# A decoder step on one core: the sample tokens' attention, one sequence at a time, between the column blocks of the first half's up projection

## The chip, the cores and the metric

The kernel runs on one core of one Trainium2 chip. The metric is the device time of one execution in microseconds (us), as a median over runs. Short names of the engines: PE is TensorE (the matmuls), PEld its weight loads, DVE VectorE, ACT ScalarE, POOL GpSimd, SP SyncE, which here only starts DMAs. Each engine works through its own list of instructions in order; an instruction that has to wait holds up all that stand behind it in that list. PSUM is the memory that matmuls write to, SBUF the one that they read from.

## What is computed

One layer of a hybrid decoder, for a prompt of 1024 tokens and for 8 sampled sequences of 4 new tokens each (32 sample tokens). Shortened:

```python
proj = x @ w_in                                    # q, k, v | HGRN2's four parts | two gates
oa = diff_attention(q, k, v)                       # prompt: causal over its own 1024 keys
# sample: over 1024 cached keys and values in pages of 128, then the 4 new ones
k_past = cache_k[page_table].reshape(Bs, past_len, N_HEADS_A, 2, HEAD_DIM_A)
v_past = cache_v[page_table].reshape(Bs, past_len, N_HEADS_A, 2 * HEAD_DIM_A)
oa = diff_attention(qa, (k_past, ka), (v_past, va), sample_masks, lam)
ob = hgrn2_scan(...)
merged = sigmoid(ga) * (oa @ w_branch_a) + sigmoid(gg) * (ob @ w_branch_b)
h = layer_norm(ALPHA * x + merged @ w_out)
a, g = split(h @ w_up)                             # 2 x 2816 columns
y = (gelu(causal_conv3(a) + b) * g) @ w_down
out = layer_norm(ALPHA * h + y)
```

`diff_attention` is the difference of two softmaxes per head, 4 heads of 2 x 64 columns. The sample tokens' attention needs nothing of the prompt, and its result is first used in the second half of the tokens (below), in `oa @ w_branch_a`.

## The kernel before

Large matmuls are float32 split into a high and a low part (`split`, lines 129 to 131: ACT writes the high part, DVE the rest), and each product is three matmuls: high by high, high by low, low by high (`mm3`, `mm3s`; lines 225 to 227 and 235 to 237). Weights come through `wunit`: SP loads 512 KB into one of two `raw` buffers (line 142), ACT makes a tile `wh`, DVE a tile `wl`, of each of which five exist.

The program runs input projection, HGRN2 and prompt attention over all tokens, and then merge, up projection, down projection for two halves of the tokens: first prompt tokens 0 to 511, then prompt tokens 512 to 1023 with the 32 sample tokens. The up projection (`ffn`) is a loop over 22 column blocks m of 128. A block takes 48 matmuls for `a` (weights `wa`), a convolution on DVE, a Gelu on ACT, 48 matmuls for the gate (`wg`), a product and a split on DVE into the pair `u`. In the first half the blocks m < 16 do two chunks of 256 tokens (96 matmuls of 128x256 per block), the others one chunk of 512 (48 of 128x512). The pairs u0 to u15 lie in the pool `up`, u16 to u21 in `f3`.

Between the first half's merge and its up projection stands `sample_attn`, for two groups of 4 sequences. In a group, for each sequence j (a key step): POOL gathers the sequence's cached keys in two page buffers `pg` of 1 MB by indirect DMA (line 713); four DVE block transposes turn them into the one buffer `pw` (line 738); 64 small matmuls of 32x256 on 32x32 tiles of the array take them against the queries `q2` (line 744), which POOL copies into place, 16 copies per group (line 730). Scores of four steps stay in four PSUM buffers. Then the softmax (lines 748 to 760), a scaling by matmul that also turns the weights (lines 766, 769), the new tokens' share (line 777), and for each sequence a value step: two gathers into `pg` or into the halves of `pw`, and 32 matmuls on 128x32 tiles (line 789; two records each). At last a norm, a transpose (line 207) and a DMA to `osc` (line 807).

The order is not written out by hand: a scheduler with its own model of time places each engine's instructions by the order of the code, by what they need and by when buffers come free. So parts of the up projection already stand between the steps of `sample_attn` in the kernel before: blocks m < 16 need none of the buffers that `sample_attn` holds. The pools are stacks at two sides of SBUF: `z` (weights of `w_out`, later rows of the layer norm), `f1` (rows of x, line 942), `ap` (all buffers of `sample_attn`) and `f3` take turns at the right side.

The last step of the merge is `turn_`: for each tile of 128 tokens 8 transposes on PE (line 207), scale and shift on DVE and ACT (lines 957, 959), and the split into `hh` and `hl` (lines 130, 131), which the up projection reads.

Of the kernel before, what the change touches and what calls it, by code (L numbers as in the profile page):

```python
# [7 lines left out]
F32 = mybir.dt.float32  # L8
# [7 lines left out]
D = 1024  # L16
KD = 8
TP = 1024
TS = 32
T = TP + TS  # L20
NT = 9
DFF = 2816
NM = 22
# [22 lines left out]
def hybrid_step(ctx: ExitStack, tc: tile.TileContext, I, O):  # L46
# [49 lines left out]
    class Slots:  # L96
        def __init__(self, n):
            self.free = list(range(n))
            self.of = {}
# [606 lines left out]
    def sample_attn(ap):  # L706
        crow = {nm: I[nm].rearrange(pat, r=4) for nm, pat in (
            ("cache_k", "a l (p r) h m d -> (a l p) (r h m d)"), ("cache_v", "a l (p r) h e -> (a l p) (r h e)"))}

        def pages(dst, nm, b, c):  # L710

            i = b * 2 + c
            G.indirect_dma_start(dst.rearrange("p r e -> p (r e)"), None, crow[nm], bass.IndirectOffsetOnAxis(ap=idx[:, i:i + 1], axis=0))

        def half():
            return ap.tile([128, 4, 512], F32, tag="pg", name="pg", bufs=2)

        def whole():
            return ap.tile([128, 8, 512], F32, tag="pw", name="pw")

        q2 = ap.tile([128, 4, 4, 160], F32, name="q2")
        G.memset(q2, 0.0)
        qw = q2.rearrange("p c h (j x) -> p c h j x", x=40)
        for g in range(2):
            for c in range(4):
                src = qsm[c * 32:c * 32 + 32, :, g * 16:g * 16 + 16].rearrange("p h (j s) -> p h j s", j=4)
                for a in range(4):
                    G.tensor_copy(qw[a * 32:a * 32 + 32, c, :, :, (c // 2) * 4:(c // 2) * 4 + 4], src)  # L730
            sc = [ps_s.tile([128, 512], F32, tag="s", name="ps_s")[:, :256] for _ in range(2)] + [pst()[:, :256] for _ in range(2)]
            for j in range(4):
                kT = whole().rearrange("p x y -> p (x y)").rearrange("p (k q t) -> p k q t", k=16, t=32)
                for f in range(2):
                    kp = half()
                    pages(kp, "cache_k", g * 4 + j, f)
                    for r in range(0, 4, 2):
                        V.transpose(kT[:, :, f * 4 + r:f * 4 + r + 2].rearrange("p k q t -> p q k t"),  # L738
                                    kp[:, r:r + 2].rearrange("p q (k t) -> p q k t", t=32))
                for c in range(4):  # L740
                    for a in range(4):
                        ra = slice(a * 32, a * 32 + 32)
                        for hh in range(4):
                            PE.matmul(sc[a][hh * 32:hh * 32 + 32], lhsT=q2[ra, c, hh, j * 32:j * 32 + 32],
                                      rhs=kT[ra, hh * 4 + c].rearrange("p q t -> p (q t)"),
                                      start=(j + c == 0), stop=(j + c == 6))
            Pg = ap.tile([128, T], F32, tag="Pg", name="Pg")
            S.copy(Pg[:, TP:T], sn[:, g])
            Pv = Pg[:, :TP].rearrange("p (q a t) -> p q a t", q=8, a=4)
            for a in range(4):  # L750
                evac("sv"[a % 2], Pv[:, :, a], sc[a].rearrange("p (q t) -> p q t", t=32))
            mx = ap.tile([128, 8], F32, tag="mx", name="mx", bufs=2)
# [6 lines left out]
            Cg = ap.tile([128, 128], F32, tag="Cg", name="Cg")  # L759
            V.tensor_scalar(Cg, selC, mx[:, 7:8], None, ALU.mult)  # L760
            aT = ap.tile([128, 8, 128], F32, tag="aT", name="aT")
# [8 lines left out]
            an = ap.tile([TS, 128], F32, tag="an", name="an")  # L770
            evac("v", an, p[:TS, :128])

            po = pst()
            pov = po.rearrange("p (j e) -> p j e", j=4)
            for hh in range(4):
                hr = slice(hh * 32, hh * 32 + 32)
                PE.matmul(pov[hr], lhsT=an[:, hr], rhs=vs_[:, None, hh * 128:hh * 128 + 128].to_broadcast([TS, 4, 128]), start=True, stop=False)
            for j in range(4):
                if j % 2:
                    w = whole()  # L780
                    vps = [w[:, :4], w[:, 4:]]
                else:
                    vps = [half(), half()]
                for f in range(2):
                    pages(vps[f], "cache_v", g * 4 + j, f)
                for q in reversed(range(8)):
                    for hh in range(4):
                        hr = slice(hh * 32, hh * 32 + 32)
                        PE.matmul(pov[hr, j], lhsT=aT[:, q, hr], rhs=vps[q // 4][:, q % 4, hh * 128:hh * 128 + 128],
                                  start=False, stop=(j == 3 and q == 0))  # L790
            osb = ap.tile([128, 128], F32, tag="osb", name="osb", bufs=2)
# [6 lines left out]
            sq = ap.tile([128, 128], F32, tag="sq", name="ssq_")  # L798
# [6 lines left out]
            oc = ap.tile([128, 4, 16], F32, tag="soc", name="soc")  # L805
# [93 lines left out]
    def load_o(th, nh):  # L899
        Ot = [hilo(up, f"u{k}") for k in range(8)]  # L900
        for k in range(8):
            raw = wide(("hs", "ae")[k % 2])
            SY.dma_start(raw[:, :nh], osc[k, :, th:th + nh])
            split(raw[:, :nh], Ot[k][0][:, :nh], Ot[k][1][:, :nh])
        return Ot

    def zt(i, dt=F32R):

        return zp.tile([128, (2, 2, 2, 1)[i], D], dt, tag=f"z{i}", name=f"z{i}")
# [94 lines left out]
    def ffn(half, th, nh, tiles, cks, H, f3):  # L1004
# [3 lines left out]
        U = []  # L1008
        for m in range(NM):
            wa, wg = w_A(w_up, m * 128), w_A(w_up, DFF + m * 128)  # L1010
# [42 lines left out]
            U.append(u)  # L1053
        lnrow, rt01, rt23, rt4 = (zt(i, F32) for i in range(4))
# [3 lines left out]
        bst = zp.tile([128, 5, KD, 6], F32, tag="bst2", name="bst2")  # L1058
# [76 lines left out]
        return ln2  # L1135

    def rpool(name):
        return tc.tile_pool(name=name, bufs=1, side="right")
# [5 lines left out]
    with rpool("z") as zp:  # L1144
        H = merge(Ot, *HALVES[0])
    with rpool("ap") as ap:
        sample_attn(ap)
    with rpool("z") as zp:
        with rpool("f3") as f3:
            ln2 = ffn(0, *HALVES[0], H, f3)  # L1150
            Ot = load_o(*HALVES[1][:2])
        ln2(0, 4)
        H = merge(Ot, *HALVES[1])
        with rpool("f3") as f3:
            ffn(1, *HALVES[1], H, f3)

# [91 lines left out]
```

## Time and profile before

| | |
|---|---|
| time, median of 3 runs | 1828.04 us (1822.92 to 1828.65) |
| the profiled execution's own time | 1826.89 us |
| its span, first to last instruction | 1825.1 us |
| mean granted TensorE clock | 0.987 |
| busy: PE, DVE, ACT, POOL | 97%, 57%, 41%, 11% of the span |
| first half's up projection starts on PE | at 826.48 us |
| `sample_attn` on PE, first to last matmul | 851.13 to 1007.17 us |
| the stretch in which both share PE | 826.48 to 1013.71 us |

Times within the trace are counted from the span's start. The granted clock is the share of TensorE's full clock (2.4 GHz) that its throttle let through; in this trace it is 1.00 or 0.50 (1.2 GHz) at any moment, and a mean in between says for how long it was the one or the other. The profile's busy time of PE counts modelled ends of matmuls, so a busy PE can still be a slow one: how fast it works is read from the number of matmuls in a stretch.

### The profile page before, as it was taken

Reading aid. Unit: us, or ns where it says so; the run is one execution under the profiler, and the core shown is the slowest. Engines: PE = TensorE matmul, PEld = TensorE weight load, DVE = VectorE, ACT = ScalarE, POOL = GpSimd, SP = SyncE. Lnnn points to the kernel's source line nnn. Section 1 sums busy time; section 2 is a strip of 40 time slices with the busy share of each in tenths; the row PEclk is TensorE's granted clock in tenths of the full one; section 3 lists DMA queues with packets and bytes.
Section 4 is the critical chain, followed back from the end, with each engine's and each line's share of the span. In section 5 each row is a group of like instructions: output and inputs, shape, how many; then the busy total and the mean of one; then the engine's idle time right before and its main releaser. Section 6 shows DMA issues by size and latency. Waiting matters only on the chain.

```text
span 1825.1 us, 33731 instructions
## 1 busy us (share of the span) xinstructions
PE 1769.4 (97%) x13652; PEld 1657.4 (91%) x13652; DVE 1036.4 (57%) x2199; ACT 747.7 (41%) x1774; POOL 200.7 (11%) x280
## 2 busy tenths in 40 slices
PE   8999999999999999998898999999899999999996
PEld 8999999999999999887687998888887999999996
DVE  5757646764656553657454555434856555554336
ACT  6466354445553544334223333323325434343223
POOL 1000110120211010003321000000500000000113
PEclk9999999999999999999889999999999999999998
DMA  6110211221211223725677433333643323232224
GB/s 203 46 60 26 82 61 41 91 62 61 87 62 64 63 67 123 255 93 175 225 259 273 124 94 93 99 96 107 210 135 93 105 82 93 84 91 85 87 88 125
DMA packets 234832, 199.37 MB, mean 109 GB/s; under 512 B 8050, under 2 KB 213106, under 8 KB 230562
## 3 DMA queue, kind: packets, MB, share of 16 engines
q1 hardware_dynamic: 218432, 140.92, 25.7%
q0 software_dynamic: 9296, 47.44, 7.0%
q10 hardware_dynamic: 6948, 8.86, 1.4%
q8 instruction: 107, 1.75, 0.4%
q14 instruction: 49, 0.40, 0.1%
HBM read 173.00 MB, written 24.19 MB: 108 GB/s over the span
## 4 chain that ended last, share of the span: by engine, by line
PE 85%; DMA 5%; DVE 5%; issue 2%; ACT 1%; POOL 1%; SPq 0%; POOLq 0%; DVEq 0%; ACTq 0%
PE mm L237 13%; PE mm L236 12%; PE mm L235 12%; PE mm L225 11%; PE mm L227 10%; PE mm L226 10%; PE tp L207 3%; DMA pg<-in_cache_k_dram,idx 3%; PE tp L662 2%; PE sb L405 2%; PE mm L246 1%; PE scp L635 1%; PE scp L634 1%; DVE pw L738 1%; PE mx L225 1%
## 5 line engine op out<-in xcount | busy, mean ns | idle before, releaser
L131 DVE TENSOR_TENSOR wl<-raw,wh 128x512 fp32r<-128x512 f32 (+1 forms) x404 | 287.8, 717 | 359.6 <-ACT wh L130 339.7
L130 ACT CAST wh<-raw 128x512 fp32r<-128x512 f32 (+1 forms) x404 | 244.8, 611 | 498.2 <-PE mm L236 389.3
L236 PE MATMUL mm<-hl,wh 128*128 128x256 f32 (+2 forms) x1312 | 386.5, 295 | 1.6 <-DVE mv L893 1.4
L235 PE MATMUL mm<-hh,wh 128*128 128x256 f32 (+2 forms) x1312 | 384.8, 294 | 3.3 <-ACT hh L130 2.7
L237 PE MATMUL mm<-hh,wl 128*128 128x256 f32 (+2 forms) x1312 | 386.9, 295 | 0.0
L235 PEld LDWEIGHTS mm<-hh,wh 128*128 128x128 f32 x1312 | 247.9, 189 | 11.1 <-ACT hh L130 3.5
L236 PEld LDWEIGHTS mm<-hl,wh 128*128 128x128 f32 x1312 | 247.4, 189 | 9.0 <-issue 2.6
L237 PEld LDWEIGHTS mm<-hh,wl 128*128 128x128 f32 x1312 | 247.5, 189 | 6.0 <-issue 1.6
L225 PE MATMUL mm<-xh,wh 128*128 128x384 f32 (+1 forms) x560 | 187.1, 334 | 0.4 <-ACT wh L130 0.3
L226 PE MATMUL mm<-xl,wh 128*128 128x384 f32 (+1 forms) x560 | 186.8, 334 | 0.0
L227 PE MATMUL mm<-xh,wl 128*128 128x384 f32 (+1 forms) x560 | 186.0, 332 | 0.0
L225 PE MATMUL mm<-wh,xh 128*128 128x256 f32 x480 | 136.5, 285 | 0.7 <-DVE rb L578 0.7
L226 PE MATMUL mm<-wl,xh 128*128 128x256 f32 x480 | 136.3, 284 | 0.2 <-DVE wl L131 0.2
L227 PE MATMUL mm<-wh,xl 128*128 128x256 f32 x480 | 135.9, 283 | 0.0
L225 PEld LDWEIGHTS mm<-xh,wh 128*128 128x128 f32 x560 | 105.4, 188 | 3.8 <-issue 2.3
L227 PEld LDWEIGHTS mm<-xh,wl 128*128 128x128 f32 x560 | 105.4, 188 | 1.8 <-issue 1.5
L226 PEld LDWEIGHTS mm<-xl,wh 128*128 128x128 f32 x560 | 105.5, 188 | 1.2 <-issue 0.8
L225 PEld LDWEIGHTS mm<-wh,xh 128*128 128x128 f32 x480 | 90.2, 188 | 1.4 <-issue 0.9
L226 PEld LDWEIGHTS mm<-wl,xh 128*128 128x128 f32 x480 | 90.4, 188 | 0.5 <-DVE wl L131 0.4
L1068 POOL TENSOR_TENSOR c<-hh,hl 128x512 f32<-128x512 f32 (+2 forms) x24 | 22.7, 948 | 616.9 <-DVE u20l L131 391.3
L227 PEld LDWEIGHTS mm<-wh,xl 128*128 128x128 f32 x480 | 90.5, 188 | 0.1
L203 ACT COPY s<-tp 128x512 f32<-128x512 f32 (+3 forms) x96 | 39.4, 426 | 100.8 <-PE tp L207 42.6
(673 smaller groups left out, 3786.9 us busy)
## 6 DMA issues: line engine op xcount, KB each, us to landing
raw<-in_w_up_dram SPq DMA_DIRECT2D x88, 512.0 KB, 3.8
raw<-in_w_in_dram SPq DMA_DIRECT2D x44, 512.0 KB, 3.9
raw<-in_w_down_dram SPq DMA_DIRECT2D x36, 512.0 KB, 3.5
raw<-in_w_out_dram SPq DMA_DIRECT2D x16, 512.0 KB, 3.6
raw<-in_w_down_dram SPq DMA_DIRECT2D x18, 384.0 KB, 3.1
gsc<-gt ACTq DMA_DIRECT2D x32, 192.0 KB, 1.9
raw<-in_w_branch_b_dram SPq DMA_DIRECT2D x16, 256.0 KB, 4.1
raw<-in_w_branch_a_dram SPq DMA_DIRECT2D x16, 256.0 KB, 4.0
```

Of the source, the lines that this page charges most:

```text
L130: S.copy(h, src)
L131: eng.tensor_tensor(l, src, h.bitcast(F32), ALU.subtract)
L203: S.copy(out, in_)
L207: PE.transpose(out, in_, ident[:n, :n])
L225: PE.matmul(ps, lhsT=ah, rhs=bh, start=(i == 0), stop=False)
L226: PE.matmul(ps, lhsT=ah, rhs=bl, start=False, stop=False)
L227: PE.matmul(ps, lhsT=al, rhs=bh, start=False, stop=(i == n - 1))
L235: PE.matmul(ps, lhsT=ah, rhs=bh, start=(k == 0), stop=False)
L236: PE.matmul(ps, lhsT=ah, rhs=bl, start=False, stop=False)
L237: PE.matmul(ps, lhsT=al, rhs=bh, start=False, stop=(k == n - 1))
L405: PE.matmul(p[:, a * 64:a * 64 + 64], lhsT=W[:, a * 128:a * 128 + 128], rhs=rhs[:, a * nb:a * nb + nb], start=True, stop=True)
L662: PE.matmul(po[:, :128], lhsT=aT[:, j * 128:(j + 1) * 128], rhs=v_[:, j], start=(j == 0), stop=(j == i))
```

## The change

`sample_attn` becomes a class with the steps as methods: `keys(b)` and `values(b)` for one sequence b of 8, `soft(g)` at the end of a group's fourth key step, `out(g)` after its fourth value step. `ffn` takes a function that it calls behind each column block; in the first half this is `beside(m)`: behind the blocks 1, 2, 4, 5, 6, 8, 9, 10 one key step each, behind the blocks 12, 13, 15, 16, 17, 19, 20, 21 one value step each.

The buffers: the page buffers `pg`, and the softmax weights `aT` and `an` of both groups (two buffers of each), lie in a new pool `av` at the left side, where `z` was, and stay to the end of the up projection; `q2` and `pw` lie in `ap` at the right side, where `f1` was, and are given back behind block 10. Values come through `pg` alone. The softmax's scores `Pg` use `pw`. `z` moves to the left side, `f3` is opened at block 16. The instructions and their number stay the same but for this: values go through page buffers in rising order of rows.

```diff
-    def sample_attn(ap):
...
-        for g in range(2):
...
-            for j in range(4):
-                kT = whole().rearrange("p x y -> p (x y)").rearrange("p (k q t) -> p k q t", k=16, t=32)
-                for f in range(2):
-                    kp = half()
-                    pages(kp, "cache_k", g * 4 + j, f)
...
-            for j in range(4):
-                if j % 2:
-                    w = whole()
-                    vps = [w[:, :4], w[:, 4:]]
-                else:
-                    vps = [half(), half()]
...
+    class SampleAttn:
...
+        def pages(self, nm, b, c):
+
+            dst = self.av.tile([128, 4, 512], F32, tag="pg", name="pg", bufs=2)
...
+        def keys(self, b):
+            g, j = b // 4, b % 4
+            q2 = self.q2
+            if j == 0:
...
+                        G.tensor_copy(qw[a * 32:a * 32 + 32, c, :, :, (c // 2) * 4:(c // 2) * 4 + 4], src)
+                self.sc = [ps_s.tile([128, 512], F32, tag="s", name="ps_s")[:, :256] for _ in range(2)] + [pst()[:, :256] for _ in range(2)]
+            kT = self.whole().rearrange("p (k q t) -> p k q t", k=16, t=32)
+            for f in range(2):
+                kp = self.pages("cache_k", b, f)
+                for r in range(0, 4, 2):
+                    V.transpose(kT[:, :, f * 4 + r:f * 4 + r + 2].rearrange("p k q t -> p q k t"),
+                                kp[:, r:r + 2].rearrange("p q (k t) -> p q k t", t=32))
...
+            if j == 3:
+                self.soft(g)
...
+        def values(self, b):
+            g, j = b // 4, b % 4
+            aT, an = self.aT[g], self.an[g]
...
+            for f in range(2):
+                vp = self.pages("cache_v", b, f)
...
+            if j == 3:
+                self.out(g)
...
-    def ffn(half, th, nh, tiles, cks, H, f3):
+    def ffn(half, th, nh, tiles, cks, H, beside=None):
...
+            if m == NU:
+                f3 = f3s.enter_context(rpool("f3"))
...
             U.append(u)
+            if beside:
+                beside(m)
...
-    with rpool("ap") as ap:
-        sample_attn(ap)
...
+    avs, aps = ExitStack(), ExitStack()
+    av = avs.enter_context(tc.tile_pool(name="av", bufs=1))
+    ap = aps.enter_context(rpool("ap"))
+    sample = SampleAttn(ap, av)
+
+    def beside(m):
+
+        i = m % 11
+        for b in range(8 * i // 11, 8 * (i + 1) // 11):
+            (sample.keys if m < 11 else sample.values)(b)
+        if m == 10:
+            aps.close()
+        if m == NM - 1:
+            avs.close()
+            open_z()
+
+    ln2, f3s = ffn(0, *HALVES[0], H, beside)
```

What the scheduler makes of it. On every engine the order is the old one up to the last tile's `turn_`, and from the first half's down projection on it is nearly the old one again: SP starts the two row loads of the layer norm (`lnrow`) a little later, behind some loads of `w_down`, and where the second half's merge meets its up projection one matmul and a few ACT and DVE instructions trade places. In between, three places.

DVE, at the end of the first half's merge: the last two tiles' scale and shift (`hs`), their low parts (`hl`), and the first key step's transposes. Before:

```order
L957 TENSOR_SCALAR hs<-ps_s,pt 128x128 x2
L131 TENSOR_TENSOR hl<-hs,hh 128x4x128 x2
L957 TENSOR_SCALAR hs<-tp,pt 128x128 x2
L957 TENSOR_SCALAR hs<-ps_s,pt 128x128 x2
L131 TENSOR_TENSOR hl<-hs,hh 128x4x128 x2
L131 TENSOR_TENSOR wl<-raw,wh 128x512 x3
L738 STREAM_TRANSPOSE pw<-pg 128x2x16x32 x2
```

and now:

```order
L974 TENSOR_SCALAR hs<-ps_s,pt 128x128 x2
L131 TENSOR_TENSOR hl<-hs,hh 128x4x128 x2
L743 STREAM_TRANSPOSE pw<-pg 128x2x16x32 x4
L974 TENSOR_SCALAR hs<-tp,pt 128x128 x2
L974 TENSOR_SCALAR hs<-ps_s,pt 128x128 x2
L131 TENSOR_TENSOR hl<-hs,hh 128x4x128 x2
L131 TENSOR_TENSOR wl<-raw,wh 128x512 x2
```

The four transposes of the first key step now stand ahead of the last tile's `hs` and `hl`; before, they stood behind them and behind three `wl`.

PE, some 60 matmuls into the up projection, behind the last tile's transposes (`mm` is the up projection's PSUM, `ps_s` and `tp` the scores'). Before:

```order
L236 MATMUL mm<-hl,wh 128x256
L237 MATMUL mm<-hh,wl 128x256
L235 MATMUL mm<-hh,wh 128x256 x2
L236 MATMUL mm<-hl,wh 128x256
L237 MATMUL mm<-hh,wl 128x256
```

and now:

```order
L236 MATMUL mm<-hl,wh 128x256
L237 MATMUL mm<-hh,wl 128x256
L749 MATMUL ps_s<-pw,q_9082 32x256 x4
L749 MATMUL tp<-pw,q_9082 32x256 x4
L749 MATMUL ps_s<-pw,q_9082 32x256 x4
L749 MATMUL tp<-pw,q_9082 32x256 x12
L235 MATMUL mm<-hh,wh 128x256 x2
L749 MATMUL ps_s<-pw,q_9082 32x256 x4
L236 MATMUL mm<-hl,wh 128x256
```

28 of the first key step's 64 matmuls moved here; before, the first of them stood 123 up matmuls later. Further on, the order lists these numbers of up matmuls between one key step's last matmul and the next one's first: before 40, 40, 46 in the first group and 40, 44, 40 in the second; now 96, 192, 96, then 110 with the softmax's matmuls among them, then 178, 96, 96. Between value steps before 57 and 31 at two places and none at the others, now 96, 192, and then 48, 48, 96, 48 and 48 of the twice as long 128x512. The sample's matmuls stand in 17 groups before and in 21 now; the softmax's matmuls have 40 and 38 up matmuls ahead of them before, now 45 and 44.

POOL, from the merge's last `lrs` (a helper of its layer norm) to the first value pages, a piece of the difference:

```order
-L364 TENSOR_TENSOR lrs<-mv,mhalf 128x1 x4
-L724 MEMSET q_9079 128x2560
-L713 DMA pg<-in_cache_k_dram,idx 128x2048 x2
-L730 COPY q_9079<-qsm 32x16x4 x16
-L713 DMA pg<-in_cache_k_dram,idx 128x2048 x6
+L364 TENSOR_TENSOR lrs<-mv,mhalf 128x1 x3
+L723 DMA pg<-in_cache_k_dram,idx 128x2048 x2
+L364 TENSOR_TENSOR lrs<-mv,mhalf 128x1
+L716 MEMSET q_9082 128x2560
+L737 COPY q_9082<-qsm 32x16x4 x16
+L723 DMA pg<-in_cache_k_dram,idx 128x2048 x8
```

The first two pages now stand ahead of the clearing of `q2`: the buffers `pg` lie where `z` was, and wait for the merge's last matmul on `z`'s last part, while `q2` and `pw` lie where `f1` was, and wait for the last tile's transposes on PE.

## Rows read from the trace of the kernel before

**Rows 1.** The page, busy time, share of the span, instructions: TensorE.

```profile
PE 1769.4 (97%) x13652; PEld 1657.4 (91%) x13652; DVE 1036.4 (57%) x2199; ACT 747.7 (41%) x1774; POOL 200.7 (11%) x280
```

**Rows 2.** The page, chain of work that ended last, share by engine.

```profile
PE 85%; DMA 5%; DVE 5%; issue 2%; ACT 1%; POOL 1%; SPq 0%; POOLq 0%; DVEq 0%; ACTq 0%
```

**Rows 3.** Windows: stretch, length, busy by engine (instructions), TensorE clock, DMA share, GB/s.

```profile
826.48:1013.71 187.23, 165.16 (x2463) 145.03 (x2463) 104.56 (x167) 59.98 (x125) 49.85 (x69) 0.93 0.67 232
1020.00:1090.00 70.00, 70.00 (x593) 70.00 (x593) 38.49 (x63) 27.95 (x63) 0.00 (x0) 1.00 0.37 108
```

**Rows 4.** Groups by shape, TensorE, 826.48 to 1013.71: busy us, mean ns, idle before.

```profile
L236 PE MATMUL mm<-hl,wh 128*128 128x256 f32 x288 | 82.8, 288 | 0.9 <-DVE mv L893 0.7 <-DVE hl L131 0.2
...
L766 PE MATMUL ps_s<-Cg,Pg 128*128 128x128 f32 x32 | 4.0, 280 | 2.1 <-ACT wh L130 1.1 <-DVE Cg L760 1.0
L777 PE MATMUL tp<-vs__71,an 32*32 32x512 f32 x16 | 2.1, 600 | 0.0
```

**Rows 5.** Windows: sample groups, up matmuls between two, two stretches at half clock.

```profile
952.13:954.81 2.68, 2.68 (x129) 1.80 (x128) 1.73 (x4) 1.12 (x2) 0.00 (x0) 1.00 0.92 341
918.24:920.12 1.88, 1.88 (x65) 1.68 (x64) 0.00 (x0) 0.38 (x1) 0.50 (x1) 1.00 1.01 423
992.54:999.49 6.95, 6.95 (x61) 6.82 (x57) 2.12 (x5) 1.86 (x3) 1.87 (x2) 1.00 0.96 364
865.06:869.64 4.58, 4.58 (x128) 2.93 (x128) 2.14 (x4) 1.14 (x2) 1.45 (x1) 0.50 0.81 261
938.49:948.73 10.24, 10.24 (x77) 6.10 (x70) 2.72 (x4) 0.65 (x2) 0.84 (x1) 0.50 0.19 53
```

**Rows 6.** Waits of TensorE, 826.4 to 1013.7: us in total, times, longest us.

```profile
PE ps_s L744 <- DVE pw L738: 11.2, 4, 6.0
PE tp L789 <- DMA pw<-in_cache_v_dram,idx: 6.1, 1, 6.1
PE mm L235 <- ACT hh L130: 1.4, 1, 1.4
...
PE ps_s L766 <- ACT wh L130: 1.1, 1, 1.1
PE ps_s L766 <- DVE Cg L760: 1.0, 1, 1.0
```

**Rows 7.** Timeline at the merge's end: start, us, instruction, idle before, releaser.

```profile
823.11 0.40 PE L227 MATMUL mm<-z,u14l 128*128 128x512 f32 x1
...
834.03 2.24 POOL L724 MEMSET q<- 128x2560 f32 x1 [5.25 <-PE ps_s L207]
...
834.36 0.73 DVE L957 TENSOR_SCALAR hs<-tp,pt 128x128 f32<-128x128 f32 x2 [2.11 <-ACT hs L959]
...
835.84 1.39 DVE L131 TENSOR_TENSOR hl<-hs,hh 128x512 fp32r<-128x512 f32 x2
...
836.43 1.08 POOL L713 DMA_INDIRECT pg<-in_cache_k_dram,idx  x1 [0.17 <-issue]
...
836.58 0.38 PE L236 MATMUL mm<-hl,wh 128*128 128x256 f32 x1 [0.22 <-DVE hl L131]
...
844.57 2.37 DVE L738 STREAM_TRANSPOSE pw<-pg 128x1024 f32<-128x1024 f32 x2 [2.29 <-DMA pg<-in_cache_k_dram,idx]
...
847.20 4.46 POOL L730 COPY q<-qsm 32x64 f32<-32x64 f32 x12 [6.82 <-DMA pg<-in_cache_k_dram,idx]
```

**Rows 8.** Tile `pg`, tile `pw`, and line 142 from 836 to 1010: issue to landing.

```profile
DMA to landing us min/median/max: 5.4/7.2/9.3
...
DMA to landing us min/median/max: 5.8/8.7/11.1
...
DMA to landing us min/median/max: 3.6/7.5/12.5
```

**Rows 9.** Groups by line, DVE and ACT, 826.48 to 1013.71: busy us, mean ns, idle before.

```profile
L738 DVE STREAM_TRANSPOSE pw<-pg 128x1024 f32<-128x1024 f32 x32 | 37.7, 1221 | 27.7 <-DMA pg<-in_cache_k_dram,idx 14.3 <-PE tp L744 13.4
...
L130 ACT CAST wh<-raw 128x512 fp32r<-128x512 f32 x35 | 21.6, 620 | 74.4 <-PE mm L236 61.6 <-DMA raw<-in_w_up_dram 12.8
```

More of the change, by code (lines that the diff above doesn't have):

```diff
@@ L747, in sample_attn, with soft @@
-            Pg = ap.tile([128, T], F32, tag="Pg", name="Pg")
+                    ra = slice(a * 32, a * 32 + 32)
+                    for hh in range(4):
+                        PE.matmul(self.sc[a][hh * 32:hh * 32 + 32], lhsT=q2[ra, c, hh, j * 32:j * 32 + 32],
+                                  rhs=kT[ra, hh * 4 + c].rearrange("p q t -> p (q t)"),
+                                  start=(j + c == 0), stop=(j + c == 6))
+            if j == 3:
+                self.soft(g)
+        def soft(self, g):
+            av = self.av
+            Pg = self.whole()[:, :T]
@@ L769, in sample_attn @@
             PE.matmul(p[:TS, :128], lhsT=Pg[:, TP:T], rhs=Cg, start=True, stop=True)
-            an = ap.tile([TS, 128], F32, tag="an", name="an")
+            an = av.tile([TS, 128], F32, tag="an", name="an", bufs=2)
             evac("v", an, p[:TS, :128])
[L773 to L777, printed above, removed]
@@ L787, in sample_attn @@
                     for hh in range(4):
                         hr = slice(hh * 32, hh * 32 + 32)
-                        PE.matmul(pov[hr, j], lhsT=aT[:, q, hr], rhs=vps[q // 4][:, q % 4, hh * 128:hh * 128 + 128],
-                                  start=False, stop=(j == 3 and q == 0))
-            osb = ap.tile([128, 128], F32, tag="osb", name="osb", bufs=2)
+                        PE.matmul(pov[hr, j], lhsT=aT[:, f * 4 + q, hr], rhs=vp[:, q, hh * 128:hh * 128 + 128],
+                                  start=False, stop=(j == 3 and f * 4 + q == 7))
@@ L792, in sample_attn, with out @@
+            if j == 3:
+                self.out(g)
+        def out(self, g):
+            av, pov = self.av, self.pov
+            osb = av.tile([128, 128], F32, tag="osb", name="osb")
+            mx = av.tile([128, 8], F32, tag="mx", name="mx", bufs=2)
             for j in range(4):
@@ L907, in zt @@
     def zt(i, dt=F32R):
-        return zp.tile([128, (2, 2, 2, 1)[i], D], dt, tag=f"z{i}", name=f"z{i}")
+        return zp[0].tile([128, (2, 2, 2, 1)[i], D], dt, tag=f"z{i}", name=f"z{i}")
     def merge(Ot, th, nh, tiles, cks):
@@ L1057, in ffn @@
         SY.dma_start(lnrow[:, 1], I["ln2_b"].to_broadcast([128, D]))
-        bst = zp.tile([128, 5, KD, 6], F32, tag="bst2", name="bst2")
+        bst = zp[0].tile([128, 5, KD, 6], F32, tag="bst2", name="bst2")
         def down(m, cs):
@@ L1143, in hybrid_step, with open_z @@
     hp = ctx.enter_context(tc.tile_pool(name="hp", bufs=1, side="right"))
[L1144 to L1155 removed]
+    zs, zp = ExitStack(), [None]
+    def open_z():
+        zp[0] = zs.enter_context(tc.tile_pool(name="z", bufs=1))
+    open_z()
+    H = merge(Ot, *HALVES[0])
+    zs.close()
+    avs, aps = ExitStack(), ExitStack()
[10 more added lines that the diff above has]
+            avs.close()
+            open_z()
+    ln2, f3s = ffn(0, *HALVES[0], H, beside)
+    Ot = load_o(*HALVES[1][:2])
+    f3s.close()
+    ln2(0, 4)
+    H = merge(Ot, *HALVES[1])
+    ffn(1, *HALVES[1], H)[1].close()
+    zs.close()
 def _consts():
```

66 lines of the change are left out of this document (32 added, 34 removed).

## The prediction

> **What bounds the kernel now.** I read the page's busy times first: TensorE works 97% of the span, no other engine more than 57% [rows 1], and the chain that ended last runs through PE for 85% of it, through DMA and DVE for 5% each [rows 2]. So time can only be won where PE waits or works slowly. The windows show where: the stretch from 826.48 to 1013.71 us, in which the sample's steps and the up projection share PE, has PE busy 165.16 of 187.23 us at a mean clock of 0.93; some undisturbed 70 us of up projection behind it run busy throughout at 1.00 [rows 3]. Those 70 us hold 593 matmuls of 128x256, 0.118 us each.
>
> How much the stretch loses follows from the work in it. It holds three times the 288 matmuls of one kind [rows 4], 864, at 0.118 us: 102.0 us. A group of one key step's 64 matmuls takes 2.68 us, a value step's 1.88 us [rows 5]; eight of each: 21.4 and 15.0 us. The softmax's and the new tokens' matmuls take 4.0 and 2.1 us [rows 4], the few that are left some 1.5. Together 146.0 us, so **41.2 us are lost**. The other way round: 22.1 us idle, of which the rows name 11.2 us at four key steps, 6.1 at one value step, 1.1 and 1.0 at the softmax, and 1.4 at the start [rows 6]; 0.07 x 187.2 = 13.1 us by half clock, in four stretches of which two are shown [rows 5]; and 17 changes between up projection and sample. Such a change costs 0.22 us: 57 up matmuls between two value steps took 6.95 us, and 57 x 0.118 is 6.73 [rows 5]. That makes 3.4, together 38.6 of the 41.
>
> Why PE waits: `pw` is one buffer, so a step's transposes (four of 1.22 us, 4.9 us of DVE) wait for the last step's matmuls, 13.4 us in all, and for pages, 14.3 us [rows 9]; a page takes 5.4 to 9.3 us to land, into `pw` up to 11.1 [rows 8]. Between two key steps of a group stand 40 to 46 up matmuls, 4.7 to 5.4 us: less than the 4.9 us and the way there and back.
>
> **The change part by part.** *Key steps.* The same instructions, but six of seven distances are now 96 to 192 up matmuls, 11.3 to 22.7 us, the seventh 110 with the softmax in it. The chain of transposes needs 4.9 us of it: 6 us to spare. The pages of a step are asked for when the transposes of the one before have freed `pg`, so over 11 us before their own transposes, against 9.3 at most [rows 8]. The four waits at L744 go, 11.2 us, and what is late next is PE itself.
>
> *Value steps.* Here each page must land, in one of two buffers, between the last step's use and the next. The distances are at least 48 matmuls of 128x512, 11.3 us at twice 0.118, and the first page is free half a group, about 1 us, before the group ends. With a 1.1 us issue on POOL [rows 7] some 11.5 us are left: above 9.3, just above the 11.1 of the slowest page of `pw` [rows 8]. I take no wait; the bounds are 0 and one of about 1 us at each of five close steps, 5 us.
>
> *Transposes and weights on DVE.* Up projection alone keeps DVE busy 38.49 of 70.00 us [rows 3], 6.2 of a block of 96 matmuls; one step adds 4.9 us and 2.7 of PE time, so 11.1 of 14.0 us, 79%. It has room, but a lump of 4.9 us stands ahead of a `wl`. Five tiles of `wl` are kept, and a tile lasts a quarter of a block or so (35 tiles for nine blocks [rows 9]), 2.8 us: 14 us of cover. Cost nothing; without that cover, 4.9 us per step. Weights themselves land in 12.5 us at worst [rows 8], already hidden now: ACT waits 12.8 us for them in the whole stretch, but 61.6 for PE [rows 9].
>
> *DMA.* The same bytes move through the 22 blocks instead of nine, so the share of 0.67 [rows 3] falls. Worth nothing on PE by itself.
>
> *The start of the up projection: an added wait.* The order puts the first step's four transposes on DVE ahead of the last tile's `hs` and `hl`. Its pages can be asked for after PE's last matmul on `z`, 823.11 [rows 7], and land by 831 to 834; but POOL clears `q2` and DVE's transposes write `pw` in the place of the rows of x, which wait for the last tile's transposes on PE, as the clearing does now (834.03 [rows 7]). So the transposes take DVE from about 834.0 to 838.8; behind them the two `hs` and `hl` (0.73 and 1.39 us [rows 7]) end at about 841.0, where they now end at 837.2. PE first reaches the key matmuls, at about 835.5, waits for `pw` until 838.8 and for the rest of `hl` to 840.9; now it goes on at 836.58 [rows 7]. Of these 4.3 us the 28 key matmuls moved here fill 1.2: **3.1 us lost**, beside the 2.2 that the start loses now (the 1.4 of [rows 6], 0.2 before 836.58 [rows 7], and pieces). Queued behind the transposes is nothing but that tile and two `wl`, of which five are in store. After the wait the clock may fall once: one of the four stretches cost 13.1/4 = 3.3 us; I take half, 1.7, bounds 0 and 3.3.
>
> *The first page earlier on POOL.* Now it is asked for at 836.43, lands for the transposes at 844.57, and the copies into `q2` wait for PE's first group (12 of them at 847.20 [rows 7]). The order moves it ahead of the clearing; what waits behind it on POOL is the clearing, which waits for PE anyway. No cost.
>
> *Softmax.* 45 and 44 up matmuls, 5.2 us, stand ahead of its matmuls, where 40 and 38, 4.6 us, left waits of 1.1 and 1.0 [rows 6]. I take 0.5 at each, 1.0; bounds 0 and 2.1.
>
> *Changes between the two.* 21 instead of 17, at the 0.2 us worked out above: 4.2 us in all. The Trainium skill says in "TensorEngine Tiling (Array Packing)", section Key Properties, that changing the tiling mode drains TensorE; that speaks against cutting the sample's work into more pieces. The row agrees that a change is not free and puts it at 0.22 us, a piece of four more at 0.9.
>
> *Layer norm rows, `out`, down projection.* The rows of the layer norm are asked for behind the last step's end instead of before; they are used at the end of the down projection. `out`'s chain after each fourth value step has 34 matmuls of 128x512, 8 us, in front of its transpose. Nothing; 1 us if that cover is too short.
>
> **Sum.** Losses left: 4.2 for changes, 5.3 for the start (2.2 and 3.1), 1.7 for its clock, 1.0 for the softmax, 12.2 us. Gain 41.2 - 12.2 = 29.0 us. The profiled execution took 1826.89 us, so 1797.9; the median of the runs shown is 1.15 above it. **Forecast 1799 us**, with the bounds (5 for values, 1.7 of clock and 1.1 of softmax either way, 1 for `out`, and 2.4 that the two accounts of the loss differ by) 1793 to 1807.
>
> **The rivals.** *Pages late.* The value steps have but a margin of 0.4 us against the slowest page into `pw`. If pages take 12.5 us, like the slowest weights [rows 8], each of the five close steps waits 1 us, and if half of the 16 steps wait 1 us and two of them let the clock fall (3.3 each), 14.6 us are lost: about 1813. For it: in the groups shown DMA stands at 0.8 to 1.01 of its engines [rows 5], and one page let PE wait 6.1 us [rows 6]. Against it: the same pages then spread over 22 blocks instead of nine, and none into `pg` took over 9.3 us [rows 8].
>
> *The gain does not come.* The waits at the steps are hidden but PE is then held by weights, as two buffers `raw` and DVE share one stretch: the 29 us are given back, 1828. ACT's 61.6 us of waiting for PE [rows 9] speaks against it. That the scheduler leaves the steps where they were is excluded by the order.
>
> *Slower.* Every key step's 4.9 us on DVE shows up on PE, since `wl` and the convolution queue behind it. The eight then cost 39 us, and with a clock that falls at half of them, 4 x 3.3, 52 us are lost beside the 29 that are won: 1799 + 52 = 1851. It decides from 3.6 us per step on (29/8). For it: DVE at 79% in these blocks, and a lump is no average. Against it: PE ran at full clock in the groups now, with transposes in the same stretches, and all waits that it had for DVE were for `pw`, none for `wl` [rows 6].
>
> **How the numbers follow.** Forecast 0.76; pages late 0.13; no gain 0.06; slower 0.05. The range needs the forecast's 1793 to 1807 and, to hold 8 in 10, most of the pages' case: up to 1816 above, and 1791 below, for a start that costs nothing. What a measurement can tell from no change is about 0.3%, 5.5 us: below 1822.5 is faster. That gives 0.89 faster (forecast and late pages), 0.06 within, 0.05 slower.
>
> **What would show it.** In the profile of the changed kernel: one wait of some 3 us at the first key matmuls (L749) and then for `hl`; none over 1 us at a later key or value step; waits under 1 us at the softmax; a mean clock of 0.98 or more from there to the end of the up projection; groups of 2.7 and 1.9 us as now; DVE waiting for PE at `wl`. It is wrong if PE waits for `wl` or `wh` (DVE or weights are the bound), if pages are what the value matmuls wait for, or if a half clock stays in several stretches.

## The result

The changed kernel takes 1802.95 us (median of 4 runs, 1801.28 to 1803.89) against 1828.35 of the kernel before beside it: a ratio of 0.9867, 95% interval 0.9847 to 0.9887, 25.4 us less. In a later group of runs the ratio was 0.9872 (0.9851 to 0.9894). The forecast was 1799 us, the range 1791 to 1816.

The page of the changed kernel, its lines for busy engines and for the chain that ended last; they answer to [rows 1] and [rows 2]:

```profile
PE 1761.8 (98%) x13652; PEld 1654.1 (92%) x13652; DVE 1035.4 (57%) x2199; ACT 747.9 (42%) x1774; POOL 200.0 (11%) x280
...
PE 89%; DVE 4%; DMA 3%; ACT 2%; issue 1%; POOL 1%; SPq 0%; POOLq 0%; DVEq 0%; ACTq 0%
```

Each of these engines has as many instructions as before. DMA's share of the chain fell from 5% to 3%, PE's rose from 85% to 89%.

To compare the two, a stretch is needed that holds the same work in both: from the first matmul of the first half's up projection to the first of its down projection, with all of the sample's attention. Windows, columns as in [rows 3]; first the kernel before:

```profile
826.48:1160.52 334.04, 311.97 (x3423) 278.73 (x3424) 184.01 (x292) 118.67 (x248) 51.96 (x71) 0.96 0.53 176
```

and now the changed one, with the eight us from its first key step on:

```profile
824.60:1135.82 311.22, 304.67 (x3421) 274.25 (x3421) 183.40 (x288) 118.68 (x247) 48.08 (x67) 0.98 0.58 186
838.00:846.00 8.00, 7.74 (x75) 5.84 (x76) 3.07 (x8) 1.85 (x3) 4.64 (x11) 0.57 0.57 185
```

22.8 us of the 23.8 between the two profiled spans are here; the stretch begins 1.9 us earlier, and what comes behind it takes 0.9 longer. (In the fourteen profiles of this document the stretch begins anywhere from 823.7 to 826.5 us, with the same matmuls ahead of it, so that this 1.9 need not come of the change.) PE's idle time fell from 22.1 to 6.6 us. By the granted clock the kernel before lost 13.7 us in four stretches at half clock (summed from windows of half a us), the changed one 5.1 in two: 3.4 around 842, where the second window shows a mean of 0.57 over 8 us, and 1.7 at the start. A second profile of the changed kernel (e9) has 5.1 again, but the 1.7 fall at the softmax there. What PE still waits for there, as in [rows 6] (the row for ACT's `hh` lies just ahead of the stretch):

```profile
PE ps_s L749 <- POOL q L737: 3.1, 1, 3.1
PE ps_s L776 <- ACT ae L203: 1.7, 1, 1.7
PE mm L235 <- ACT hh L130: 1.4, 1, 1.4
PE mm L236 <- DVE mv L910: 0.7, 1, 0.7
PE mm L235 <- DVE c L1071: 0.6, 1, 0.6
PE ps_s L776 <- DVE Cg L770: 0.5, 1, 0.5
```

Of the sample's steps only the first key step and the softmax wait, and the up projection waits once, 0.6 us, for the first block's product with the gate (L1071); at the seven later key steps and the eight value steps no wait is left. Windows of 192 up matmuls, a key step, a value step and 96 up matmuls, columns as in [rows 3] and answering to [rows 5]:

```profile
876.92:899.84 22.92, 22.92 (x197) 22.79 (x192) 15.59 (x23) 8.73 (x21) 2.08 (x2) 1.00 0.50 166
914.08:916.85 2.77, 2.77 (x130) 1.99 (x129) 0.58 (x2) 0.44 (x1) 1.62 (x8) 1.00 0.86 244
1016.99:1018.87 1.88, 1.88 (x68) 1.68 (x65) 1.02 (x2) 0.29 (x1) 0.50 (x1) 1.00 0.34 101
1018.87:1030.43 11.56, 11.56 (x101) 11.43 (x97) 4.22 (x7) 3.31 (x9) 1.39 (x2) 1.00 0.72 236
```

96 up matmuls at 0.118 us are 11.33; the 11.56 between two steps hold 0.23 us for the change of work, the price that the prediction took from a row of before. The Trainium skill's drain at a change of tiling mode ("TensorEngine Tiling (Array Packing)", Key Properties) is compatible with that, and at 0.23 us apiece it did not decide anything.

The start went as follows (timeline, columns as in [rows 7]; DVE):

```profile
833.43 4.62 DVE L743 STREAM_TRANSPOSE pw<-pg 128x1024 f32<-128x1024 f32 x4 [3.06 <-PE ps_s L207]
...
838.58 0.72 DVE L974 TENSOR_SCALAR hs<-ps_s,pt 128x128 f32<-128x128 f32 x2
839.41 1.33 DVE L131 TENSOR_TENSOR hl<-hs,hh 128x512 fp32r<-128x512 f32 x2
```

and PE:

```profile
838.26 0.42 PE L749 MATMUL ps_s<-pw,q 32*32 32x256 f32 x4 [3.08 <-POOL q L737]
```

The profile names POOL's copies into `q2` as what released PE, and these run from 835.83 to 841.14; the transposes end 0.2 us before PE's start, at 838.05. Which of the two held PE can't be told here; e7 below tells it. The last tile's `hl` follows at 840.7, while PE, at half clock, is still in the key matmuls, so it costs nothing more.

### The profile page after: what moved, and what is told of

It reads as the page before. It is cut to its first block, busy times and chain, and to the rows that moved or that the text cites. A ratio compares the mean times of both kernels' runs of the same rounds, so it can differ in the third digit from the quotient of the medians.

```text
span 1801.3 us, 33741 instructions
## 1 busy us (share of the span) xinstructions
PE 1761.8 (98%) x13652; PEld 1654.1 (92%) x13652; DVE 1035.4 (57%) x2199; ACT 747.9 (42%) x1774; POOL 200.0 (11%) x280
## 4 chain that ended last, share of the span: by engine, by line
PE 89%; DVE 4%; DMA 3%; ACT 2%; issue 1%; POOL 1%; SPq 0%; POOLq 0%; DVEq 0%; ACTq 0%
PE mm L236 14%; PE mm L235 14%; PE mm L237 14%; PE mm L225 11%; PE mm L227 10%; PE mm L226 10%; PE tp L207 3%; PE tp L662 2%; PE sb L405 2%; PE mm L246 1%; PE scp L635 1%; PE scp L634 1%; PE mx L225 1%; PE mx L227 1%; DMA c<-gsc 1%
## 5 line engine op out<-in xcount | busy, mean ns | idle before, releaser
L235 PEld LDWEIGHTS mm<-hh,wh 128*128 128x128 f32 x1312 | 249.2, 190 | 13.7 <-issue 4.1
```

Source lines behind the costliest of these rows:

```text
L235: PE.matmul(ps, lhsT=ah, rhs=bh, start=(k == 0), stop=False)
```

## The experiments

All times are medians, beside runs of the kernel before in the same group; the changed kernel's 1802.7 to 1803.0 us and 0.9867 to 0.9872 are the mark.

| run | us | ratio to before, 95% interval |
|---|---|---|
| e1 both kinds of step bunched | 1815.3 | 0.9931 (0.9915 to 0.9946) |
| e2 key steps bunched | 1810.5 | 0.9914 (0.9899 to 0.9929) |
| e3 value steps bunched | 1806.8 | 0.9883 (0.9868 to 0.9898) |
| e4 first step behind `hl` | 1798.1 | 0.9839 (0.9826 to 0.9852) |
| e5 before, copies on ACT | 1821.3 | 0.9974 (0.9960 to 0.9988) |
| e6 e4, and softmax a block later | 1794.2 | 0.9816 (0.9797 to 0.9834) |
| e7 six transposes | 1823.3 | 0.9981 (0.9969 to 0.9993) |
| e8 six transposes on e6 | 1812.9 | 0.9931 (0.9909 to 0.9953) |
| e9 the changed kernel again | 1802.7 | 0.9872 (0.9851 to 0.9894) |
| e10 e8, three raw buffers | 1791.8 | 0.9815 (0.9797 to 0.9832) |
| e11 e6, three raw buffers | 1794.6 | 0.9827 (0.9811 to 0.9843) |
| e12 e6 again | 1792.5 | 0.9820 (0.9801 to 0.9839) |

### Are the distances the reason? (e1 to e3)

The new buffers stay, and the steps of a group are handed over together again. e1 in `beside`:

```diff
-        i = m % 11
-        for b in range(8 * i // 11, 8 * (i + 1) // 11):
-            (sample.keys if m < 11 else sample.values)(b)
+        for b in {1: (0, 1, 2, 3), 6: (4, 5, 6, 7)}.get(m, ()):
+            sample.keys(b)
+        for b in {12: (0, 1, 2, 3), 17: (4, 5, 6, 7)}.get(m, ()):
+            sample.values(b)
```

e2 has only the first of the two tables, e3 only the second; the other steps lie as in the changed kernel.

> The changed kernel with its buffers, but the steps of a group handed over together: keys of sequences 0 to 3 behind block 1, 4 to 7 behind block 6, values behind 12 and 17. Up matmuls between key steps are then 62, 45, 40 and 48, 47, 43 instead of 96 to 192, between value steps 52 to 83 of 128x256 or 35 of 128x512 instead of 96 and more. Theory A (the distances between the steps won the time, by covering transposes and pages): the waits at the key matmuls and at the value matmuls come back, 8 to 20 us with half clock behind them, so 1812 to 1825 us. Theory B (the buffers and the earlier first pages won it): no wait comes back, 1803 us give or take 3.

> Only the key steps handed over together (behind blocks 1 and 6), value steps as in the changed kernel. Theory A: the waits for pw come back, some 8 us with one or two stretches at half clock, 1810 to 1816 us. Theory B: 1803 us. If the key steps carry all of the gain and the value steps none, the time is that of the kernel in which both are handed over together.

> Only the value steps handed over together (behind blocks 12 and 17), key steps as in the changed kernel. Theory A: a page is asked for about 1 us ahead of a group's end and lands 7.7 us after its issue, and 35 matmuls of 128x512 are 8.2 us, 52 to 65 of 128x256 6.1 to 7.7 us: waits for pages of 1 to 3 us at six steps, and one or two stretches at half clock, 1808 to 1814 us. Theory B: 1803 us.

Measured: 1815.3, 1810.5 and 1806.8 us. PE's waits in e1, from the start of the up projection to its end:

```profile
PE ps_s L749 <- DVE pw L743: 7.2, 3, 2.8
PE ps_s L749 <- POOL q L737: 3.1, 1, 3.1
...
PE tp L800 <- DMA pg<-in_cache_v_dram,idx: 1.2, 2, 0.7
```

The waits for `pw` come back, and half clock costs 10.2 us instead of 5.1. But 1815.3 is only half the way back: distances are worth about 12.4 of the 25.4 us. Of these the key steps carry some 7.5 (e2 against the mark). The value steps carry little: e3 lies 3.8 us above the mark, but its interval overlaps the changed kernel's, and in the profiles the part from the first matmul of the value steps to the end of the up projection is only 1.6 us longer in e3 (1018.82 to 1140.27, 121.4 us) than in the changed kernel (1016.00 to 1135.82, 119.8); the rest lies ahead of the first value step, where the two kernels have the same steps. Theory B, that the distances do nothing, falls; theory A, that they do everything, falls too. The value steps' part was expected at 5 to 11 us. In e3 no wait for a page is left: its 35 matmuls of 128x512, 8.2 us, just suffice. In e1, at the same distances, 0.7 us are waited behind 51 matmuls of 128x256 and 0.5 behind 35 of 128x512. So the margin at 48 matmuls, 11.2 us, is about 2.5 us and not the 0.4 of the prediction.

### What else the new order removed (e5)

The other half must lie in what e1 kept. POOL's list of the kernel before, around the copies into `q2`, shows where to look:

```profile
851.93 1.12 POOL L713 DMA_INDIRECT pg<-in_cache_k_dram,idx  x1 [0.27 <-POOL q L730]
...
892.88 4.72 POOL L730 COPY q<-qsm 32x64 f32<-32x64 f32 x11 [5.21 <-DMA pg<-in_cache_v_dram,idx]
897.87 0.97 POOL L713 DMA_INDIRECT pw<-in_cache_v_dram,idx  x1 [0.27 <-POOL q L730]
```

Twelve of the copies wait 6.8 us for the pages just asked for ([rows 7], 847.20), and the second key step's pages are asked for only behind them; eleven copies of the next group do the same ahead of the second value step's pages. PE's two longest waits, 6.0 and 6.1 us in [rows 6], are these two steps. (What ties copies that neither read nor write pages to the pages' landing is not shown.) In the changed kernel both first pages are asked for over 12 us ahead of the copies and have landed. e5 takes the copies off POOL in the kernel before, and PE's order stays the same:

```diff
-                    G.tensor_copy(qw[a * 32:a * 32 + 32, c, :, :, (c // 2) * 4:(c // 2) * 4 + 4], src)
+                    S.copy(qw[a * 32:a * 32 + 32, c, :, :, (c // 2) * 4:(c // 2) * 4 + 4], src)
```

> The kernel before, with the copies into q2 (two times 16) on ACT instead of POOL; PE's order stays word for word the same, with 40 to 46 up matmuls between key steps. Theory C: in the kernel before, the two longest waits of PE (6.0 us at the second key step, 6.1 us at the second value step) come from POOL's list and not from the distances: twelve copies wait there for pages just asked for, and the next pages are asked for only behind the copies (851.9 and 897.9 us). Then both waits shrink to 2 us or less, and the half clock behind each (3.4 us) goes: 1808 to 1817 us. Theory A (distances alone): the pages are late because 40 matmuls are too few, wherever the copies run: 1823 to 1828 us.

Measured: 1821.3 us, 5.8 less than before; between the two expectations. POOL's second pair of pages and PE's waits in e5:

```profile
849.04 0.96 POOL L713 DMA_INDIRECT pg<-in_cache_k_dram,idx  x1 [8.86 <-DVE pw L738]
```

```profile
PE ps_s L744 <- DVE pw L738: 7.9, 4, 2.7
PE ps_s L766 <- ACT wh L130: 3.1, 1, 3.1
...
PE tp L207 <- DVE osb L802: 1.4, 1, 1.4
```

The mechanism is shown: both long waits are gone (the key step waits 2.7 us, the value step 0.3). The price is not what they had in the trace. Other key steps wait now, and the softmax waits 3.1 us instead of 1.1. Half clock still costs 10.2 us of the 13.7, half of it in one long stretch, 10 us around 939, where the first group's `out` waits for its transpose, as in [rows 5] at 938.49. And groups that wait for no other engine take longer: the fourth key step 3.4 us instead of 3.0, the second group's first two value steps together 4.8 instead of 3.6, with holes of about half a us between matmuls for which the trace shows no wait; what makes them stays open. In e1 the long stretch is missing, and 5.1 us of clock with it. Copies and this stretch would together make up some 11 of the other 13 us; the stretch was not tested by itself, nor were the other buffers that e1 keeps.

### The start (e4)

```diff
             kT = self.whole().rearrange("p (k q t) -> p k q t", k=16, t=32)
+            if b == 0:
+                V.tensor_copy(kT[:, 0, 0:8:2, 0], H[1][:, 7, 508:512].bitcast(F32))
```

> The changed kernel with one more DVE instruction of 128x4 elements, which reads the last tile's hl and writes into pw ahead of the first key step's transposes, so that these stand behind the last hl; the first key matmuls then stand 120 up matmuls into the up projection instead of 60. Theory: the wait of 3.1 us at the first key matmuls and the half clock behind it (3.4 us) are caused by the transposes standing ahead of the last tile's hs and hl; both go, 1796 to 1798 us. Rival: it is POOL's copies into q2, which run from 835.8 to 841.1 us, or the pages, that hold the first step; then PE waits as long, only later, and the time stays at 1802 to 1804 us.

Measured: 1798.1 us. The wait at the first key matmuls and the half clock behind it are gone, as the theory said. It doesn't decide against the rival, though: the copies into `q2` are over at 838.97 in e4, and the first key matmul stands at 841.70, so they could hold nothing up there. The waits of PE that are left:

```profile
PE ps_s L778 <- DVE Cg L772: 4.8, 2, 3.9
PE mm L235 <- ACT hh L130: 1.4, 1, 1.4
PE mm L236 <- DVE mv L912: 0.7, 1, 0.7
PE mm L236 <- DVE hl L131: 0.2, 1, 0.2
```

The gain is 4.7 us rather than 6 because the softmax now waits 4.8 us instead of 2.2, 3.9 of them in the first group, which has 42 up matmuls ahead of it here instead of 45, with a half clock of 3.4 behind them.

### The softmax (e6, e12)

Why the softmax waits is seen on ACT and DVE; timelines of the changed kernel:

```profile
916.41 0.62 ACT L130 CAST wh<-raw 128x512 fp32r<-128x512 f32 x1 [3.85 <-DMA raw<-in_w_up_dram]
...
917.46 0.21 ACT L758 COPY pw<-sn 128x32 f32<-128x32 f32 x1
```

```profile
917.06 0.69 DVE L131 TENSOR_TENSOR wl<-raw,wh 128x512 fp32r<-128x512 f32 x1 [2.40 <-ACT wh L130]
...
918.32 0.41 DVE L201 COPY pw<-ps_s 128x256 f32<-128x256 f32 x1
```

The key matmuls end at 916.85, but ACT has stood since 912.6 in front of a weight that has not landed, and the scores' copies stand behind it: on ACT they start 0.6 us behind the key matmuls, on DVE, behind this weight's `wl` and a `u5l`, 1.5 us, and the softmax needs both. In the second group, with 44 matmuls of cover, both start 0.2 us behind them (at 990.20), and PE waits 0.5 us instead of 1.7. e6 keeps e4's gate and hands over the part from `Cg` on (`soft2`) a block later, so that 96 up matmuls stand ahead of it; `q2` and `pw` are given back a block later too:

```diff
+        if m in (6, 11):
+            sample.soft2()
```

> The changed kernel with the first step's transposes behind the last hl (one more DVE instruction of 128x4 elements), and with the second half of the softmax, from Cg on, handed over one block later: 96 up matmuls ahead of its matmuls instead of 42 and 40 in the kernel that has only the first of the two. Theory: what that kernel still loses at the softmax (3.9 and 1.0 us of waiting, one stretch of half clock at 3.4 us) is the softmax's chain on ACT and DVE, held up there behind a weight that lands late; 96 matmuls, 11.3 us, cover it: 1788 to 1792 us. Rival: the chain then delays the next key step, or the weight that lands late holds PE itself: 1796 to 1800 us.

Measured: 1794.2 us, and 1792.5 us in the repetition:

> The kernel with the first step behind the last hl and the softmax one block later, beside the two with a third raw buffer: 1791 to 1796 us, no wait of PE between the start of the up projection and its end.

PE's waits in e6, whole stretch:

```profile
PE mm L235 <- ACT hh L130: 1.5, 1, 1.5
PE mm L236 <- DVE mv L916: 0.7, 1, 0.7
PE mm L236 <- DVE hl L131: 0.2, 1, 0.2
PE mm L235 <- issue: 0.2, 1, 0.2
```

and its window, columns as above:

```profile
825.10:1126.69 301.59, 300.36 (x3421) 271.63 (x3421) 182.36 (x289) 117.33 (x247) 45.96 (x67) 0.99 0.59 192
```

None of the sample's steps waits any more. This version beats both kernels: 0.9816 to 0.9820 against 0.9867 to 0.9872. It also gives the price of all work in the stretch with next to no loss, 301.6 us, so the kernel before lost 32.4 us against it. (In e12, which has no half clock at the start, the stretch takes 299.7.)

### How much of DVE is free? (e7, e8, e10, e11)

The prediction put the step's 4.9 us on DVE at nothing. e7 makes the lump larger in the changed kernel:

```diff
-                for r in range(0, 4, 2):
+                for r in (0, 2, 0):
                     V.transpose(kT[:, :, f * 4 + r:f * 4 + r + 2].rearrange("p k q t -> p q k t"),
```

> The changed kernel with six transposes per key step instead of four (two of them done twice), 2.4 us more of DVE in each of eight steps. Forecast's theory: five tiles of weights ahead and 96 matmuls between steps cover a lump of 7.3 us as they cover 4.9; only the first step, which stands ahead of the last tile's hl, shows its 2.4 us, with half clock behind it perhaps: 1803 to 1810 us. Rival (DVE's lumps show up on PE): 8 times 2.4 us and half clock, 1820 to 1830 us.

Measured: 1823.3 us, 20 us more, in the range of the rival, and more than 8 times 2.4. PE's waits:

```profile
PE ps_s L776 <- DVE Cg L770: 8.0, 2, 6.1
PE mm L235 <- ACT hh L130: 5.7, 2, 4.2
PE ps_s L749 <- DVE pw L743: 3.1, 1, 3.1
PE mm L235 <- DVE c L1071: 2.5, 1, 2.5
```

They are not spread over eight steps: start, softmax and one key step have them. The scheduler also moved the softmax up, to 39 matmuls behind the key step instead of 45, so a part of the 20 us comes of that order. e8 therefore makes the same edit in e6, where start and softmax have cover.

e7 also tells what held the first key step in the changed kernel. In e7 the copies are over at 840.21, the last transpose ends at 841.42, and PE starts 0.2 us behind the transpose, as it did there:

```profile
835.66 4.55 POOL L737 COPY q<-qsm 32x64 f32<-32x64 f32 x16
839.06 2.36 DVE L743 STREAM_TRANSPOSE pw<-pg 128x1024 f32<-128x1024 f32 x2
841.62 0.68 PE L749 MATMUL ps_s<-pw,q 32*32 32x256 f32 x8 [1.57 <-issue]
```

So the transposes hold it. How much sooner PE could start if only the copies were in its way is not shown.

> Six transposes per key step instead of four (two done twice), now in the kernel whose first step stands behind the last hl and whose softmax has 96 up matmuls of cover. In the changed kernel the same 2.4 us per step cost 20 us, at three kinds of places: the start, the softmax and one ordinary key step. Theory D (a lump on DVE costs only where a chain through DVE has no cover, as at the start and the softmax): here it costs 0 to 4 us, 1794 to 1798 us. Rival (DVE is full in blocks with a step, 6.2 and 7.3 of 14.0 us or 96%, and the delay adds up from step to step): waits at the later ones of steps in neighbouring blocks, 10 to 19 us, 1804 to 1813 us.

> The changed kernel unchanged, beside the run of the same call, so that differences of a few us are compared on one chip: 1801 to 1805 us by every theory, with one wait of 3.1 us at the first key matmuls, and half clock behind it.

Measured: 1812.9 us, 19 above e6, while the unchanged kernel of e9 stood at 1802.7. Theory D falls: ordinary steps wait too. But DVE isn't full either. ACT's waits in e8, columns as in [rows 6]:

```profile
ACT wh L130 <- DMA raw<-in_w_up_dram: 42.8, 12, 6.6
```

and the chain at the eighth key step, which waited 3.8 us (timeline of ACT and of DVE):

```profile
987.20 0.63 ACT L130 CAST wh<-raw 128x512 fp32r<-128x512 f32 x1 [6.56 <-DMA raw<-in_w_up_dram]
987.73 0.61 ACT L130 CAST u9h<-c 128x512 fp32r<-128x512 f32 x1
```

```profile
987.86 0.69 DVE L131 TENSOR_TENSOR wl<-raw,wh 128x512 fp32r<-128x512 f32 x1 [6.52 <-ACT wh L130]
988.47 0.68 DVE L131 TENSOR_TENSOR u9l<-c,u9h 128x512 fp32r<-128x512 f32 x1
989.07 6.87 DVE L745 STREAM_TRANSPOSE pw<-pg 128x1024 f32<-128x1024 f32 x6
```

DVE stood idle for 6.5 us here. A `wl` behind the last lump read its `raw` late, so its buffer came free late, the next weight landed late, ACT stood in front of it with `u9h` behind, `u9l` came late on DVE, and the transposes stand behind `u9l`. If so, a third raw buffer must take the cost away. e10 gives e8 one (4 KB per partition in `av`, used in turn; `osb` takes over the buffers of `an` for the room), e11 the same to e6:

```diff
     def wraw():
+        if more[0]:
+            more[1] += 1
+            if more[1] % 3 == 0:
+                return more[0].tile([128, 1024], F32, tag="raw3", name="raw3")
         return wp.tile([128, 1024], F32, tag="raw", name="raw")
```

> The kernel with six transposes per key step, the first step behind the last hl and the softmax one block later (1812.9 us), now with three buffers for raw weights instead of two while the first half's up projection runs. Theory E (the lump on DVE costs by way of the raw buffers: a wl behind the transposes frees its buffer late, the next weight lands late, ACT stands 6.6 us in front of it with the u behind, and the next transposes start late): ACT's waits for raw fall from 42.8 us to under 15, the waits at the key matmuls to under 1 us each, 1795 to 1801 us. Theory F (DVE itself is full in blocks with a step): the third buffer changes little, 1808 to 1813 us.

> The kernel with the first step behind the last hl and the softmax one block later, four transposes, and three buffers for raw weights in that stretch. PE waits there for nothing but the start already, so by theories E and F alike the third buffer changes nothing on PE: the time of that kernel in this call, give or take 2 us, though ACT's waits for raw fall.

Measured: e10 1791.8 us, 21 less than e8, with the same distances between the steps from the second one on, and no more than e6 with four transposes; e11 1794.6, e12 1792.5 beside it, so nothing for e6, as both theories had it. In e10:

```profile
ACT wh L130 <- DMA raw<-in_w_up_dram: 2.2, 2, 1.9
```

and PE waits for no key step at all:

```profile
PE mm L241 <- ACT hh L130: 2.1, 3, 1.3
PE mm L242 <- DVE hl L131: 0.8, 2, 0.6
```

Theory E is shown: DVE has room for 7.3 us per step; what lacks is a raw buffer. The Trainium skill advises in "Trainium Kernel Development and Optimization", section Best Practices, to double-buffer for performance. That is done here; a third buffer decided 21 us once the lump was larger, and nothing while it was small.

## Why the prediction was right, point by point

**Where the time was lost: right.** 41.2 us were put on the stretch. e6, without waits at any step, is 32.4 us faster there; with the 4 to 5 us for changes of work, 1.7 at half clock and 1.1 of waiting at the start that e6 still holds, that is about 40.

**Key and value steps no longer wait: right, the reason only half.** No later key step and no value step waits. But the prediction explained the four waits at L744 and the one at L789 by too short a distance alone. The step that failed is "Why PE waits": the two longest of them, 12.1 of 17.3 us, come mostly from POOL's list; with the copies off it 3.0 are left of the 12.1 (e5). The rows had it: the copies at 847.20 with 6.82 us of waiting, read in the prediction as waiting for PE's first group, are released by DMA. The forecast survived it because the new order happens to cure both, and that is luck; distance alone accounts for some 12 us (e1).

**The start: right in its wait, short in its clock.** PE waited 3.1 us behind the first step's transposes, as the mechanism has it (e7), and without them ahead of `hs` and `hl` it doesn't (e4). That the figure agrees to the tenth is chance: the forecast's 3.1 was a wait of 3.3 us for `pw` and a shorter one for `hl`, less what the moved matmuls fill and what the start lost before. The wait for `hl` didn't come, since the key matmuls at half clock took longer, though `hs` and `hl` took 2.7 us behind the transposes and not 2.1 (one of two pairs of `hs` had been left out). That half clock cost 3.4 us, and another 1.7 fell at the start: 5.1 against 1.7 taken, and above its bound of 3.3. This is the largest mis-sized term, and half clock in several stretches was one of the prediction's own signs of being wrong.

**The softmax: mis-sized.** 2.2 us instead of 1.0, just above the upper bound of 2.1, and 1.7 of it in one wait. 45 matmuls are no cover for a chain that begins 1.5 us late behind a weight (ACT waited 3.85 us for it).

**DVE's lumps at nothing: right in size, wrong in its cover.** Five tiles of `wl`, 14 us, were named as the cover. No `wl` was waited for even with six transposes, but the two raw buffers gave out first (e8, e10). ACT's wait for weights was 12.8 us in [rows 9] and was read as hidden; in the changed kernel it is twice that:

```profile
ACT wh L130 <- DMA raw<-in_w_up_dram: 25.0, 8, 5.5
```

The row to read was what stands behind such a wait in ACT's list.

**Value pages: right at nothing**, with 2.5 us of margin (e1, e3).

**Sum.** 29.0 us were forecast, 22.8 came in the stretch. Missing are 3.4 of clock, 1.2 of softmax, 0.6 at the first block's product with the gate (L1071), some 0.7 at a key step with 3.33 instead of 2.68 us, and about 1.5 of the loss before, which the first account had too high. In the other direction 1.4 us of the start's 2.2 lie ahead of the stretch. Two slips in the prediction's own sums weigh nothing here: 17 changes at 0.22 us make 3.7 and not 3.4, and its bounds, added up, reach from 1794 to 1810 and not from 1793 to 1807. The rivals didn't come: pages are waited for nowhere. Lumps on DVE, the slower one's cause, can cost what it feared, though by way of the raw buffers: e7 shows that the changed kernel stood 2.4 us per step from losing some 20 of its 25 us.

## What to carry to other kernels

When small work is to be laid between matmuls, count for each step what stands ahead of it in every engine's list, ACT's and POOL's too: here copies behind a gather, and a weight that landed late in front of the scores' copies, set waits of PE beside those that the distance set. Cover is as deep as the shallowest buffer of the chain: five tiles of converted weights didn't help while two raw buffers fed them. And a wait of 1 to 4 us on PE has to be priced with the half clock that may follow it.

## What was not expected of the hardware

The same two waits at the start of the up projection, 1.4 and 0.7 us or nearly so, have a stretch at half clock behind them in six of the fourteen profiles and none in the other eight (the kernel before among these); it costs 1.7 us where it falls. Behind the wait of 3.1 us at the first key matmuls, 3.4 were lost by the clock in all five profiles that have it (the changed kernel twice, e1 to e3). Elsewhere the length of the wait does not tell the price: in e4 3.9 us of waiting cost 3.4, in e8 3.8 cost 1.7, and in the kernel before and in e5 a stretch of 10 us at half clock, 5.1 us lost, stands at a wait of 1.1 and 1.4 us. All these losses are half the time at half clock; a matmul of 128x256 takes 0.213 us there (the changed kernel, 826.4 to 828.5) instead of 0.118, so about a tenth less is lost by the matmuls.
